# Attention stage of a hybrid decoder trunk: TensorE's products and turnings pinned to the program's order, new planner costs, k turned ahead of q

## The chip, the cores and the metric

The kernel runs on one core of a Trainium2 chip. The metric is the device time of one execution in microseconds (us), as the median of several runs. Lower is better.

## What is computed

Two layers on x of 512 positions by 1024. Each layer is a gated feed-forward block, a mixer and another gated feed-forward block; the mixer of layer 0 is a causal differential attention with 8 heads, that of layer 1 a chunked spatial gate. All is float32. Only the attention matters here:

```python
def _diff_attention(h, w_in, w_out, q_norm, k_norm, lq1, lk1, lq2, lk2, subln, lam_init):
    q, k, v = jnp.split(h @ w_in, ...)                 # 512 x 1024 each
    q = _rmsnorm(q.reshape(B, S, H, 2, d), q_norm) * (d ** -0.5)   # d = 64, two halves a head
    k = _rmsnorm(k.reshape(B, S, H, 2, d), k_norm)
    for i in range(S // Q_BLOCK):                      # 4 blocks of 128 queries
        L = (i + 1) * Q_BLOCK
        s = jnp.einsum('bqhcd,bkhcd->bhcqk', q_blk, k[:, :L])
        p = jax.nn.softmax(jnp.where(mask, s, -jnp.inf), axis=-1)
        a = p[:, :, 0] - lam * p[:, :, 1]
        outs.append(jnp.einsum('bhqk,bkhe->bqhe', a, v[:, :L]))
    o = _rmsnorm(o, subln) * (1.0 - lam_init)
    return o.reshape(B, S, DIFF_V_WIDTH) @ w_out
```

## The kernel before, in words

x lies transposed in SBUF, 8 tiles of 128 x 512. To keep float32 precision every operand is cut into a high and a low half, and each product is made of three matmuls (high x high, low x high, high x low): `mm3`, which calls `matmul` at L135. The stages follow one another: feed-forward f0, attention, f1, f2, spatial gate, f3.

The attention stage (`attention`, from L594) consists of tasks, each a Python generator that issues some instructions and then yields what it thinks they cost. For a pair of heads `hp` there is a projection of q and k (`qk_block`: 96 matmuls of 512 columns through `project`, which yields after every six), a norm (`qk_norm`), and for every head h:

- `qk_turn` (task t): q and k of the head are turned by TensorE, four 128 x 128 turnings into one bank of PSUM for q and one for k. ScalarE and VectorE copy them out as high and low halves, two copies on ScalarE for q and four for k.
- `scores` (s, once for each block i of 128 queries): for each of the two halves `cc` one bank, two matmuls of 128 to 512 columns and, after those of both halves, one that adds the mask; then a maximum (L740) and its scaling (L742) on VectorE, an exponential (L747) on ScalarE, and the combination of both halves (L752 to L754) on VectorE.
- `turn` (e): the combined block is turned, i + 1 turnings; ScalarE copies it out.
- `values` (p): products with v.
- `head_norm` (n) and `head_turn` (o): the head's norm and the turning of its output.

Two blocks of v (`v_block`) and the out-projection (`out_part`, task w, one for a pair of heads, 48 matmuls of 512 columns) use the same banks `pp` as the projections. PSUM has 8 banks: 4 `pp`, 3 `ps` in a ring (for turnings and scores), 1 `po` (for the values).

The order in which the program issues all this comes from a planner, `interleave`. It goes through the list of tasks and takes the first whose conditions hold and whose time has come by its own clock; the list has all tasks of the heads first, in the order p, e, s for each block, and the projections last. A condition "<s0.1" means that the task was issued; one without "<" that its whole chain of work is done by the planner's clock. HOP is what it adds between engines. The costs stand in the yields. If nothing is ready, the clock jumps on. For a score step the condition reads

```python
tasks.append((f"s{h}.{i}", [f"t{h}"] + [f"<e{t}" for t in at(2 * NT)]
              + [f"<s{t}" for t in at(1)], scores(h, i)))
```

The program's order is not the order that runs. A scheduler of the compiler sorts each engine's instructions by what it takes to be ready first. Only an instruction on which `tc.keep_in_program_order` is called stays behind the instruction that precedes it on its engine in the program. `matmul` calls it while the list `fixed` is not empty. That is so in the feed-forward stages (`ffn` appends to it), and not in the attention stage; there `scores` pins the mask products and all but the first of its four products by hand. `Weights.use` splits weights into halves up to three half blocks ahead and issues their loads on SP's queue.

Of the kernel before, what the change touches and what calls it, by code (L numbers as in the profile page):

```python
# [17 lines left out]
P = 128  # L18
S = 512
NT = S // P  # L20
D = 1024
# [29 lines left out]
RSTD_AT = (3, 5, 3, 3)  # L51
STEPS = ("A0 t0 h0 B0", "A1 t1 h1 B1", "P1 A2 t2 A3 Q5", "P6 B2 B3 r3 h2 h3")
FIRST_STEPS = ("", "A0 t0 h0 B0", "A1 t1 h1 B1", "A2 B2", "P1 A3 B3 r2 r3 Q5", "P6 r4 r5 h2 h3 h4 h5")
HOP = 0.2
END = "end"


# [1 line left out]
def kernel(  # L59
# [23 lines left out]
    nc = tc.nc  # L83
# [9 lines left out]
    def bank(name, tag="ps"):  # L93
# [4 lines left out]
    ident = const.tile([P, P], F32, name="ident")  # L98
    make_identity(nc, ident)
    ident_b = const.tile([P, P], BF16, name="ident_b")  # L100
    make_identity(nc, ident_b)
    mask_b = const.tile([P, P], BF16, name="mask_b")
    nc.gpsimd.memset(mask_b, 0.0)
    nc.gpsimd.affine_select(
        out=mask_b, in_=mask_b, compare_op=ALU.is_ge, fill=MASK, base=0,
# [24 lines left out]

    fixed = []

    def matmul(ps, stationary, moving, start, stop, more=False):

        mm = nc.tensor.matmul(ps, stationary, moving, start=start, stop=stop, skip_group_check=more)  # L135
        if fixed:
            tc.keep_in_program_order(mm)

    def mm3(ps, sh, sl, mh, ml, start, stop, more=False):
        matmul(ps, sh, mh, start, False, more)  # L140
# [425 lines left out]
            else:  # L566
                state[name] = t + HOP if wait is True else max(now, wait or 0.0)

    def project(weights, p, nm, norm, rr, taken):


        ps = [bank(f"{nm}p{n}", "pp") for n in range(NT)]

        def products(k, n):
            wh, wl = weights.parts[p + k // 2]
            c0, t0 = slice(k % 2 * 512, (k % 2 + 1) * 512), slice(n * P, (n + 1) * P)
            mm3(ps[n], norm.xh[k][:, t0], norm.xl[k][:, t0], wh[:, c0], wl[:, c0], k == 0, k == KT - 1)

        for k in range(KT - 2):
            if k % 2 == 0:  # L580
                yield from weights.use(p + k // 2)
            for n in range(NT):
                products(k, n)
                if n % 2 == 1:
                    yield 1.3, [], False
        if not rr:
            rr["r"] = norm.rstd()
        yield from weights.use(p + 3)
        for n in range(NT):
            products(KT - 2, n)  # L590
            products(KT - 1, n)
            yield 1.3, taken(n, ps[n]), False

    def attention(norm, nxt):  # L594
        with ExitStack() as c:
# [21 lines left out]
            srcs, where = [], {}  # L617
# [6 lines left out]
            weights = Weights(srcs)  # L624
# [3 lines left out]
            def qk_block(hp):  # L628

                nm = f"qk{hp}"  # L630
                ssqs[hp] = stat.tile([P, NT, 8], F32, tag="ssq", name=nm + "ssq")

                def taken(n, ps):
                    sq = stat.tile([P, S], F32, tag="sq", name=f"{nm}sq{n}")
                    nc.scalar.activation(sq, ps, AF.Square)
                    qks[hp, n] = a2.tile([P, 512], F32, tag="qk", name=f"{nm}n{n}", bufs=QK_BUFS)
                    nc.scalar.activation(qks[hp, n], ps, AF.Copy)
                    nc.vector.reduce_sum(ssqs[hp][:, n, :], sq.rearrange("p (g d) -> p g d", d=HD), axis=AX.X)
                    return [("A", 1.0), ("D", 0.6)]

                yield from project(weights, where["qk", hp], nm, norm, rr, taken)

            def v_block(b):

                vts[b] = a2.tile([P, NT, 512], F32, tag="vt", name=f"vt{b}", bufs=2)

                def taken(n, ps):
                    nc.scalar.activation(vts[b][:, n, :], ps, AF.Copy, scale=rr["r"][:, n:n + 1])
                    return [("A", 0.6)]

                yield from project(weights, where["v", b], f"v{b}", norm, rr, taken)

            def qk_norm(hp):
                nm = f"qk{hp}"
# [38 lines left out]
            def qk_turn(h):  # L693
                nm, hp, hh = f"qk{h}", h // 2, h % 2
                qs, khs, kls = stacks[h % 2]
                for j in (hh, 2 + hh):
                    pt = bank(f"{nm}t{j}")
                    for n in range(NT):
                        nc.tensor.transpose(pt[:, n * P:(n + 1) * P], qks[hp, n][:, j * P:(j + 1) * P], ident)
                    for c, own in enumerate(rows):  # L700
                        other = rows[1 - c]
                        if j < 2:
                            nc.scalar.activation(qs[c][own], pt[own], AF.Copy)
                            nc.vector.tensor_tensor(qs[c][other], pt[own], f32(qs[c][own]), op=ALU.subtract)
                        else:
                            nc.scalar.activation(khs[c][own], pt[own], AF.Copy, scale=kg[own])
                            nc.scalar.activation(khs[c][other], pt[own], AF.Copy, scale=kg[own])
                            nc.vector.scalar_tensor_tensor(
                                kls[c][own], pt[own], kg[own], f32(khs[c][own]), op0=ALU.mult, op1=ALU.subtract
                            )  # L710
                    if j < 2:
                        yield 0.44, [("A", 1.1), ("D", 1.4)], False
                    else:
                        yield 0.44, [("A", 2.2), ("D", 1.4)], END

            def scores(h, i):

# [7 lines left out]
                pss = [bank(f"{nm}s{i}{cc}") for cc in range(2)]  # L725
                for cc in range(2):
                    for ks in (khs, kls):
                        mm = nc.tensor.matmul(
                            pss[cc][:, :L], qs[cc][:, i * P:L], ks[cc][:, :L], start=ks is khs, stop=False
                        )  # L730
                        if cc > 0 or ks is kls:
                            tc.keep_in_program_order(mm)
                for cc in range(2):
                    tc.keep_in_program_order(
                        nc.tensor.matmul(pss[cc][:, i * P:L], ident_b, mask_b, start=False, stop=True)
                    )
                for cc in range(2):
                    ps = pss[cc]
                    mx = stat.tile([P, 2], F32, tag="mx", name=f"{nm}m{i}{cc}", bufs=8)
# [15 lines left out]
                es[h, i] = ee[0]  # L755
                yield (
                    (0.5, 0.54, 0.76, 0.97)[i],
                    [("D", 0.7 + 0.27 * i), ("A", 0.86 + 0.22 * i), ("D", 0.4), ("D", 0.25 + 0.13 * i)], END,
                )

            def turn(h, i):
                nm, L = f"a{h}", (i + 1) * P
                e = es.pop((h, i))
                pt = bank(f"{nm}at{i}")
                for j in range(i + 1):
                    nc.tensor.transpose(pt[:, j * P:(j + 1) * P], e[:, j * P:(j + 1) * P], ident)
                at = a2.tile([P, L], F32, tag=f"at{i}", name=f"{nm}atT{i}", bufs=1)
                nc.scalar.activation(at, pt[:, :L], AF.Copy)
                ats[h, i] = at
                yield 0.11 * (i + 1), [("A", 0.25 + 0.09 * i)], END  # L770

            def values(h, i):
                at = ats.pop((h, i))
                if i == 0:
                    ocs[h] = bank(f"a{h}o", "po")
                for j in range(i + 1):
                    nc.tensor.matmul(
                        ocs[h][:, i * P:(i + 1) * P], at[:, j * P:(j + 1) * P],
                        vts[h // 4][:, j, h % 4 * P:(h % 4 + 1) * P],
                        start=(j == 0), stop=(j == i),  # L780
                    )
                yield 0.22 * (i + 1), [], END

# [22 lines left out]
            def head_turn(h):  # L806
                nm, on = f"a{h}", ons.pop(h)
                pt = bank(nm + "ot")
                for n in range(NT):
                    nc.tensor.transpose(pt[:, n * P:(n + 1) * P], on[:, n, :], ident)  # L810
                oh = a2.tile([P, S], F32R, tag="oh", name=nm + "oh", bufs=O_BUFS)
                ol = a2.tile([P, S], F32R, tag="ol", name=nm + "ol", bufs=O_BUFS)
                nc.scalar.activation(oh, pt, AF.Copy, scale=sg)
                nc.vector.scalar_tensor_tensor(ol, pt, sg, f32(oh), op0=ALU.mult, op1=ALU.subtract)
                outs[h] = (oh, ol)
                yield 0.44, [("A", 0.57), ("D", 0.66)], END

            def out_part(hp):
                last = order[-1] == ("w", hp)
                for m in range(KT):  # L820
# [9 lines left out]
                    nc.vector.tensor_tensor(x[m], pt, x[m], op=ALU.add)  # L830
                    if last:
                        nxt.add(m)
                        yield 1.3, [("D", 0.6), ("A", 1.1), ("D", 1.3)], False
                    else:
                        yield 1.3, [("D", 0.6)], False

            tasks = []
            for hp in range(4):
# [17 lines left out]
            for w, i in order:  # L856
                if w == "w":
                    tasks.append((f"w{i}", [f"o{2 * i}", f"o{2 * i + 1}"] + prev, out_part(i)))
                else:
                    tasks.append((f"{w}{i}", prev, qk_block(i) if w == "qk" else v_block(i)))  # L860
                prev = [f"{w}{i}"]
            interleave(tasks)

    def gmlp(norm, nxt):
        with ExitStack() as c:
# [230 lines left out]
```

## Time and profile before

| | us |
|---|---|
| median of 3 runs | 1932.28 (1931.55 to 1933.58) |
| the profiled execution, whole time | 1931.58 |
| its span in the trace | 1929.9 |
| TensorE busy in the span | 1913.3 |
| VectorE busy | 1329.0 |
| ScalarE busy | 902.2 |
| attention stage, first to last product | 251.9 |

Engines: PE is TensorE's matmuls, PEld its weight loads, DVE VectorE, ACT ScalarE. A product's busy time is longer than its distance to the next one, since products are pipelined; the distance between two starts tells the pace. Numbers ahead of a row of the timeline are its start and its duration in us, counted from the span's start. Names are those of the program: a2s are the scores of head 2, qk2t the turned q or k of head 2, k1l the low half of the k of an odd head, qk2p the projection of the third pair (heads 4 and 5).

### The profile page before, as it was taken

What the parts mean: (1) busy time and instruction counts of PE and PEld (TensorE: products, weight loads), DVE (VectorE), ACT (ScalarE), POOL (GpSimd) and SP (SyncE); (2) the same over time, 40 slices, a digit from 0 to 9 for tenths busy, and PEclk for the clock granted to TensorE, in tenths of its full rate; (3) what the DMA queues carried; (4) which work ended last, traced back from release to release, by engine and by line L of the source; (5) the groups of instructions that cost most, each with busy time, mean ns of one, the idle gap of its engine ahead of it and who ended that gap; (6) DMA issues with size and microseconds to landing.
All of it is one profiled execution on the core that took longest, in us unless ns stands there. A gap on an engine that the chain in (4) does not pass through costs nothing.

```text
span 1929.9 us, 29295 instructions
## 1 busy us (share of the span) xinstructions
PE 1913.3 (99%) x11490; PEld 1701.5 (88%) x11490; DVE 1329.0 (69%) x2151; ACT 902.2 (47%) x1394; POOL 63.2 (3%) x81
## 2 busy tenths in 40 slices
PE   8999999999999999999999999999999999999999
PEld 7889898877778889899889999988888888999997
DVE  7857574778888957566696666755595569665763
ACT  6535353566764635354454444543332245343541
POOL 0000000000000000000000000000000000000000
PEclk9999999999999999999999999999999999999999
DMA  6354562422122455554435545543333234454542
GB/s 211 97 143 134 131 149 80 133 66 66 55 66 88 104 137 129 137 145 125 120 99 140 142 133 142 133 135 110 107 109 95 88 109 105 136 137 137 133 125 82
DMA packets 88985, 227.51 MB, mean 118 GB/s; under 512 B 10000, under 2 KB 43152, under 8 KB 88848
## 3 DMA queue, kind: packets, MB, share of 16 engines
q1 hardware_dynamic: 78768, 188.95, 31.0%
q0 software_dynamic: 10080, 36.70, 11.5%
q8 instruction: 90, 1.47, 0.3%
q14 instruction: 47, 0.39, 0.1%
HBM read 223.52 MB, written 2.10 MB: 117 GB/s over the span
## 4 chain that ended last, share of the span: by engine, by line
PE 95%; DVE 2%; ACT 2%; issue 0%; DMA 0%; SPq 0%; ACTq 0%
PE f3dp L135 6%; PE f0dp L135 6%; PE f2dp L135 6%; PE f1dp L135 6%; PE gup L135 5%; PE gop L135 5%; PE f0p L135 3%; PE aop L135 2%; PE f3p L135 2%; PE f2p L135 2%; PE gv0p L135 1%; PE qk0p L135 1%; PE qk1p L135 1%; PE gv1p L135 1%; PE gv2p L135 1%; PE gv3p L135 1%
## 5 line engine op out<-in xcount | busy, mean ns | idle before, releaser
L490 DVE SCALAR_TENSOR_TENSOR x<-f3dp,x 128x512 f32<-128x512 f32 x32 | 22.1, 691 | 60.5 <-PE f3dp L135 60.5
L490 DVE SCALAR_TENSOR_TENSOR x<-f1dp,x 128x512 f32<-128x512 f32 x32 | 22.1, 690 | 49.2 <-PE f1dp L135 49.2
L490 DVE SCALAR_TENSOR_TENSOR x<-f2dp,x 128x512 f32<-128x512 f32 x32 | 22.1, 689 | 49.2 <-PE f2dp L135 49.2
L490 DVE SCALAR_TENSOR_TENSOR x<-f0dp,x 128x512 f32<-128x512 f32 x32 | 22.1, 690 | 48.8 <-PE f0dp L135 48.8
L987 DVE TENSOR_TENSOR x<-gop,x 128x512 f32<-128x512 f32 x24 | 16.5, 689 | 20.0 <-PE gop L135 20.0
L967 ACT ACTIVATE gh<-gut 128x512 fp32r<-128x512 f32 x16 | 10.1, 633 | 42.9 <-DVE gut L966 42.9
L830 DVE TENSOR_TENSOR x<-aop,x 128x512 f32<-128x512 f32 x32 | 21.3, 683 | 2.0 <-PE aop L135 1.9
L962 DVE TENSOR_TENSOR gst<-gs,bs 128x512 f32<-128x512 f32 x16 | 11.0, 686 | 8.8 <-PE gs L957 8.8
L957 PEld LDWEIGHTS gs<-wT,gv 128*128 128x128 f32 x128 | 16.1, 191 | 0.9
L957 PE MATMUL gs<-wT,gv 128*128 128x128 f32 x128 | 16.2, 274 | 0.0
L907 ACT ACTIVATE gv<-gv 128x512 f32<-128x512 f32 x16 | 10.1, 629 | 12.4 <-DVE gv L906 12.3
L926 DVE TENSOR_TENSOR gut<-gup,n4rbs 128x512 f32<-128x512 f32 x16 | 11.0, 685 | 6.6 <-PE gup L135 6.6
L927 ACT ACTIVATE gut<-gut,sm 128x512 f32<-128x512 f32 x16 | 11.5, 719 | 6.7 <-DVE gut L926 6.6
L968 DVE TENSOR_TENSOR gl<-gut,gh 128x512 fp32r<-128x512 f32 x16 | 11.0, 687 | 4.2 <-ACT gh L967 4.2
L266 POOL DMA_DIRECT2D f1w2b<-in_gate_up_dram x1 | 0.9, 865 | 358.7 <-DVE f1w2t L262 358.7
L942 DVE SCALAR_TENSOR_TENSOR gv<-gv,lnmv,lng 128x512 f32<-128x512 f32 x16 | 11.5, 742 | 1.5 <-DMA lng<-in_ln_g_dram 1.5
L943 DVE SCALAR_TENSOR_TENSOR gv<-gv,lny,lnb 128x512 f32<-128x512 f32 x16 | 11.6, 746 | 1.3 <-DMA lnb<-in_ln_b_dram 1.3
L266 POOL DMA_DIRECT2D f3w2b<-in_gate_up_dram x1 | 0.9, 877 | 354.2 <-DVE f3y L356 354.2
L467 ACT ACTIVATE f1g<-f1g 128x512 f32<-128x512 f32 x9 | 5.7, 633 | 14.3 <-DVE f1g L465 14.3
L467 ACT ACTIVATE f3g<-f3g 128x512 f32<-128x512 f32 x9 | 5.7, 633 | 14.3 <-DVE f3g L465 14.3
L467 ACT ACTIVATE f2g<-f2g 128x512 f32<-128x512 f32 x9 | 5.7, 633 | 14.3 <-DVE f2g L465 14.3
L966 DVE TENSOR_TENSOR gut<-gut,gst 128x512 f32<-128x512 f32 x16 | 11.0, 689 | 0.7
(20715 smaller groups left out, 8029.5 us busy)
## 6 DMA issues: line engine op xcount, KB each, us to landing
f0d<-in_down_dram SPq DMA_DIRECT2D x48, 192.0 KB, 2.5
f1d<-in_down_dram SPq DMA_DIRECT2D x48, 192.0 KB, 2.5
f2d<-in_down_dram SPq DMA_DIRECT2D x48, 192.0 KB, 2.5
f3d<-in_down_dram SPq DMA_DIRECT2D x48, 192.0 KB, 2.7
f0gu<-in_gate_up_dram SPq DMA_DIRECT2D x10, 512.0 KB, 4.9
f1gu<-in_gate_up_dram SPq DMA_DIRECT2D x8, 512.0 KB, 3.5
f2gu<-in_gate_up_dram SPq DMA_DIRECT2D x8, 512.0 KB, 3.6
f3gu<-in_gate_up_dram SPq DMA_DIRECT2D x8, 512.0 KB, 3.6
```

The source lines that it names most:

```text
L135: mm = nc.tensor.matmul(ps, stationary, moving, start=start, stop=stop, skip_group_check=more)
L467: nc.scalar.activation(g[:, 2:, :], g[:, 2:, :], AF.Silu)
L490: nc.vector.scalar_tensor_tensor(x[m], pt, 0.5, x[m], op0=ALU.mult, op1=ALU.add)
L830: nc.vector.tensor_tensor(x[m], pt, x[m], op=ALU.add)
L926: nc.vector.tensor_tensor(ut, ps, rr["rb"], op=ALU.mult)
L927: nc.scalar.activation(ut, ut, AF.Gelu, bias=sm[:, C_BU + c:C_BU + c + 1])
L942: nc.vector.scalar_tensor_tensor(vv, vv, mv[:, n, 0:1], gr, op0=ALU.subtract, op1=ALU.mult)
L943: nc.vector.scalar_tensor_tensor(vv, vv, rr["y"][:, n:n + 1], lr, op0=ALU.mult, op1=ALU.add)
L957: nc.tensor.matmul(ps[:, n * P:(n + 1) * P], v32[n][:, c * P:(c + 1) * P], wT[:, g, :], start=True, stop=True)
L962: nc.vector.tensor_tensor(t.rearrange("p (n t) -> p n t", t=P), ps.rearrange("p (n t) -> p n t", t=P), bs[:, g, :].unsqueeze(1).broadcast_ ...
L966: nc.vector.tensor_tensor(ut, ut, t, op=ALU.mult)
L987: nc.vector.tensor_tensor(x[m], pt, x[m], op=ALU.add)
```

## The change

It pins every matmul and every turning of the attention stage to the program's order: `fixed` is filled around `interleave(tasks)`, products and turnings all go through `pin`. The planner's HOP and the costs in the yields of the attention stage grow, the six matmuls of a projection to STEP = 1.37. `qk_turn` turns k first and then q. No instruction is added or taken away.

```diff
-HOP = 0.2
+HOP = 0.3
+STEP = 1.37
@@
-    def matmul(ps, stationary, moving, start, stop, more=False):
-
-        mm = nc.tensor.matmul(ps, stationary, moving, start=start, stop=stop, skip_group_check=more)
+    def pin(mm):
+
         if fixed:
             tc.keep_in_program_order(mm)
+
+    def matmul(ps, stationary, moving, start, stop, more=False):
+
+        pin(nc.tensor.matmul(ps, stationary, moving, start=start, stop=stop, skip_group_check=more))
+
+    def turned(out, src):
+        pin(nc.tensor.transpose(out, src, ident))
@@ qk_block
-                    return [("A", 1.0), ("D", 0.6)]
+                    return [("A", 1.25), ("D", 0.7)]
@@ qk_turn
-                for j in (hh, 2 + hh):
+                for j in (2 + hh, hh):
                     pt = bank(f"{nm}t{j}")
                     for n in range(NT):
-                        nc.tensor.transpose(pt[:, n * P:(n + 1) * P], qks[hp, n][:, j * P:(j + 1) * P], ident)
+                        turned(pt[:, n * P:(n + 1) * P], qks[hp, n][:, j * P:(j + 1) * P])
@@
-                        yield 0.44, [("A", 1.1), ("D", 1.4)], False
+                        yield 0.44, [("A", 1.3), ("D", 1.4)], END
                     else:
-                        yield 0.44, [("A", 2.2), ("D", 1.4)], END
+                        yield 0.44, [("A", 2.5), ("D", 1.5)], False
@@ scores
-                        mm = nc.tensor.matmul(
-                            pss[cc][:, :L], qs[cc][:, i * P:L], ks[cc][:, :L], start=ks is khs, stop=False
-                        )
-                        if cc > 0 or ks is kls:
-                            tc.keep_in_program_order(mm)
+                        matmul(pss[cc][:, :L], qs[cc][:, i * P:L], ks[cc][:, :L], ks is khs, False)
@@
-                    [("D", 0.7 + 0.27 * i), ("A", 0.86 + 0.22 * i), ("D", 0.4), ("D", 0.25 + 0.13 * i)], END,
+                    [("D", 0.9 + 0.27 * i), ("A", 1.28 + 0.22 * i), ("D", 0.5), ("D", 0.28 + 0.15 * i)], END,
@@ out_part
-                        yield 1.3, [("D", 0.6), ("A", 1.1), ("D", 1.3)], False
+                        yield STEP, [("D", 0.7), ("A", 1.25), ("D", 1.45)], False
                     else:
-                        yield 1.3, [("D", 0.6)], False
+                        yield STEP, [("D", 0.7)], False
@@ end of attention
+            fixed.append(1)
             interleave(tasks)
+            fixed.pop()
```

The turnings and products of `turn`, `values` and `head_turn` are changed in the same way as those of `qk_turn` and `scores`, and `qk_block` and `v_block` hand STEP to `project`.

## Rows read from the trace of the kernel before

**Rows 1.** The page: busy time of the engines, and the chain's shares by engine.

```profile
PE 1913.3 (99%) x11490; PEld 1701.5 (88%) x11490; DVE 1329.0 (69%) x2151; ACT 902.2 (47%) x1394; POOL 63.2 (3%) x81
PE 95%; DVE 2%; ACT 2%; issue 0%; DMA 0%; SPq 0%; ACTq 0%
```

**Rows 2.** Busy time in the attention stage; columns as in the first line.

```profile
core 0: us, PE busy (x) PEld busy (x) DVE busy (x) ACT busy (x) POOL busy (x), PEclk, DMA share, GB/s
356.20:608.10 251.90, 246.35 (x1306) 199.63 (x1306) 202.30 (x571) 160.44 (x318) 0.00 (x0) 1.00 0.22 68
```

**Rows 3.** The chain in order of time: start, us, unbroken run of one group.

```profile
420.25 0.77 PE a0at L766 x7
...
432.91 6.85 PE qk1p L135 x30
...
441.59 8.16 PE qk2p L135 x36
```

**Rows 4.** Products of projections (L135) in the four score groups: busy (count).

```profile
394.90:417.86 22.96, 16.83 (x64) 11.38 (x64) 1.00 0.22 70
457.18:479.55 22.37, 16.45 (x62) 10.85 (x61) 1.00 0.23 69
503.37:526.00 22.63, 17.57 (x66) 11.53 (x65) 1.00 0.24 71
538.78:565.32 26.54, 15.67 (x55) 9.55 (x54) 1.00 0.20 60
```

**Rows 5.** Timeline of TensorE in the second group: score products (L728) and masks.

```profile
460.19 0.36 PE L728 MATMUL a2s<-k0h,q0h 128*128 128x256 f32 x1 [1.33 <-DVE k1l L708]
...
461.45 0.38 PE L728 MATMUL a2s<-k0h,q0l 128*128 128x256 f32 x1
...
461.79 0.28 PE L735 MATMUL a2s<-mask_b,ident_b 128*128 128x128 bf16 x2
...
463.73 0.34 PE L728 MATMUL a2s<-k0h,q0l 128*128 128x384 f32 x1
...
466.75 0.50 PE L728 MATMUL a2s<-k0h,q0l 128*128 128x512 f32 x1
```

**Rows 6.** Timeline of VectorE and ScalarE in the same stretch.

```profile
462.05 0.42 DVE L740 TENSOR_REDUCE a2m<-a2s 128x1 f32<-128x256 f32 x1
...
462.58 0.20 DVE L742 TENSOR_SCALAR a2m<-a2m,qk1rq 128x1 f32<-128x1 f32 x1
...
466.79 1.22 DVE L128 TENSOR_TENSOR aqk31s0l<-aqk31r,aqk31s0h 128x1024 fp32r<-128x1024 f32 x1
...
462.88 0.57 ACT L747 ACTIVATE a2e<-a2s,a2m,qk1rq 128x256 f32<-128x256 f32 x1 [1.04 <-DVE a2m L742]
```

**Rows 7.** Busy time of all engines in the second group, columns as in rows 2.

```profile
457.18:479.55 22.37, 21.04 (x110) 16.08 (x108) 19.47 (x61) 16.33 (x40) 0.00 (x0) 1.00 0.23 69
```

**Rows 8.** Timeline of the turnings of heads 2 and 3 and their copies.

```profile
449.60 1.03 PE L699 MATMUL qk2t<-ident,qk1n 128*128 128x128 f32 x8
450.23 0.59 ACT L703 ACTIVATE q0h<-qk2t 64x512 fp32r<-64x512 f32 x1 [2.10 <-PE qk2t L699]
...
451.41 0.69 ACT L707 ACTIVATE k0h<-qk2t,kg 64x512 fp32r<-64x512 f32 x1
...
453.74 0.63 PE L699 MATMUL qk3t<-ident,qk1n 128*128 128x128 f32 x4
```

**Rows 9.** Timeline at the stage's end: the last turning and its two copies.

```profile
596.93 0.63 PE L810 MATMUL a7ot<-ident,a7on 128*128 128x128 f32 x4
597.60 0.69 ACT L813 ACTIVATE a7oh<-a7ot,sg 128x512 fp32r<-128x512 f32 x1 [0.30 <-PE a7ot L810]
...
598.48 0.74 DVE L814 SCALAR_TENSOR_TENSOR a7ol<-a7ot,sg,a7oh 128x512 fp32r<-128x512 f32 x1
```

**Rows 10.** Timeline of TensorE at the start of the kernel.

```profile
5.67 0.63 PE L135 MATMUL f0p<-n0x0l,w00wh 128*128 128x512 f32 x1
6.10 0.63 PE L135 MATMUL f0p<-n0x0h,w00wl 128*128 128x512 f32 x1
...
9.49 0.40 PE L135 MATMUL f0p<-n0x1l,w00wh 128*128 128x512 f32 x1
```

## What the change was predicted to do

> **What bounds the kernel now.** The page comes first: TensorE is busy 99% of the span and carries 95% of the chain that ended last [rows 1]. The second view is the busy time of the attention stage, whose products run from 356.2 to 608.1 us: 251.9 us, TensorE busy 246.35 of them [rows 2]. That looks as if no more than 5.5 us were to be had. So the third thing to read is the pace of unbroken runs: 36 products of 512 columns in 8.16 us, 0.227 each, and seven turnings in 0.77, 0.11 each [rows 3]. The stage has 768 products of 512 columns (174.1 us), 176 turnings and 160 value products at 0.11 (37), and 32 score steps for which the planner's own figures give 2.77 per head (22.2). That is 234 us, so 18 of the 252 are waits and joints, and 18 is the most that any order of TensorE's work could give back.
>
> The Trainium skill says the same of such a row: in "Trainium Kernel Development and Optimization", section "Performance Expectations", it calls matmul busy time a bad metric because matmuls are pipelined. By the busy row the most to be gained would be 5.5 us; by the pace it is 18, and the trace agrees with the page.
>
> The fourth view is what TensorE does while the scores run, in four groups (heads 0 and 1, 2 and 3, 4 and 5, 6 and 7). Each of the first three takes 22.4 to 23.0 us, and between the score steps lie 64, 62 and 66 products of the projections (55 of the out-projection in the last, 26.5 us) [rows 4]. So a group holds only 5.5 us of score work; the rest is filler.
>
> **The order that the change fixes.** The program's order has to be read out of the planner. At each step it takes the first task in its list that is ready, and the projections stand last in the list. A score step of a head needs its turned halves, and of the score step before it only that it was *issued* (the "<" in its conditions). So as soon as a pair's halves count as ready, s0 to s3 of one head are issued behind one another, and soon those of the other head. Banks of PSUM don't occur in the planner. Worked through with the new costs, the first pair reads: 48 products of v0, turnings k, q, k, q, 24 products, four score steps, 6 products, four score steps, 12 products, then the turnings of e0, e1 and so on among 6 to 24 products each. The other pairs are alike (with the last: four score steps, p4 and e5, four score steps, then 48 products). The old costs give nearly the same (36 products before the first turning, no filler at all between the two heads). The trace bears the reading out at places where nothing waits: 36 products before the turnings of head 2, and exactly 30 between those of a0 and a1's outputs [rows 3]. But in the score groups the trace holds 62 to 66 products where the program's order has none. In the kernel before only the later products of a score step are pinned; projections float into its waits. The change forbids that.
>
> **Score groups.** A score step takes two banks of a ring of three. Its second half therefore waits until the exponential of the step before has freed its first bank. The round can be seen in the trace: second half at 461.45, the masks at 461.79, maximum at 462.05, its scaling at 462.58, exponential at 462.88 for 0.57, and the second half of the next step at 463.73: 2.28 us [rows 5, 6]. The next round is 3.02 us [rows 5], but foreign work stands in it and behind it: squares on ScalarE, weight splits of 1.22 on VectorE [rows 6]. Without these I take 1.75, 2.28, 2.5 and 2.6 us for the four rounds of a head (an estimate: the round that is seen, its maximum and exponential shortened or lengthened by the width). For eight steps from first product to last mask that is 1.85 + 2.28 + 2.5 + 2.6 + 1.75 + 2.28 + 2.5 + 0.7 = 16.5 us; VectorE is busy 19.5 of 22.4 us in such a group [rows 7]; without the three splits in it 15 to 16 stay. That will stretch the rounds here and there, and I take 17.5. The bounds are 15 (VectorE's share alone) and 22.4 (as now, with the foreign work in it).
>
> Of the 22.96, 22.37 and 22.63 us of the first three groups, all filler but 6 products is pushed behind the group: 58 x 0.227 = 13.2, 12.7 and 13.6 us. What is left of them is 9.8, 9.7 and 9.0. In their place stands 17.5: 52.5 - 28.5 = **+24.0** (bounds +16.5 and +38.7). In the last group 26.54 - 55 x 0.227 = 14.1 is left; in its place come two runs of four steps (1.85 + 2.28 + 2.5 + 0.7 = 7.3 each), 30 value products and turnings (3.3) and 0.5 for their banks: 18.5, **+4.4** (bounds +4 and +12.6). Behind the waiting score product all of TensorE is queued; nobody else waits for the filler, which is why nothing gives the time back.
>
> **Turnings, k ahead of q.** No instruction is added. There are four turned blocks and three banks, so the last block (q of the second head) waits for the first bank, which is now that of k: four copies on ScalarE at 0.69 (the first copy begins 0.63 after the turning does in the trace [rows 8]), about 3.45 us after the start, and 1.3 us of other turnings lie in between. So 2.15 us are bare. In the trace the fourth block starts 4.14 us after the first [rows 8], and 11 floated products cover it; with that wait 2.85 would be bare. I take 2.4, of which 0.4 are there now: **+8** for four pairs (bounds +6.8 and +10). That k comes first helps no one: a score step needs both.
>
> **The end.** After the last turning (596.93) the halves of head 7 are done at 599.2 [rows 9]: 2.3 us. Turning (0.44) and the three products of head 6 that may run (0.68) leave **+1.2**; now floated products cover it.
>
> **The rest.** The costs and STEP change landmarks only; products stand there that wait for nothing. The loads on SP and the weight splits move with the projections by a few steps. Three halves are split ahead, and 24 products of one half are 5.4 us of cover. Fewer joints and small waits elsewhere: from -8 (nearly half of the 18 us) to +2; I take -1.
>
> **Sum.** 24.0 + 4.4 + 8 + 1.2 - 1 = +36.6 us on the profiled execution's own 1931.58: **1968**. (Its span is 1929.9; the median of the runs shown, 1932.28, lies 0.7 above it.) Bounds: +20 and +63, 1951 to 1995.
>
> **Rivals.**
> *The clock falls too: 1987, chance 0.10.* In the first microseconds of the kernel products of 512 columns stand 0.43 us apart instead of 0.227 [rows 10], which is the lower of the two levels (1.2 against 2.4 GHz), until about 9.5 us: ten products at 0.2 too much, 2 us lost. If four groups with bare waits brought this level back, each would lose between those 2 us and its own work once more (6.9): +8 to +28, I take +18. Against it: the granted clock is 1.00 throughout the stage although waits of 1.3 us occur in it [rows 2, 5]. The Trainium skill, "TensorE: Matmul & The Clock Gate", section "A second HAM failure mode: psum-queue depth-cycling", describes just this: short idling between groups while PSUM banks are cycled lets the clock go back and forth. No run here shows it.
>
> *The order saves waits: 1922, chance 0.12.* Of the 18 us of waits and joints, over half could go if the planner's order put the products where the waits are. It decides in the score groups: filler between score steps must be 1.3 us or more in each round. For it: the costs of the softmax steps grow, which makes the planner hold back what depends on them, and a wait like that of 1.33 us for a bank [rows 5], which 24 products ahead of it don't cover now, could be met by an order that knows the longer copies. Against it: a successor score step depends on the issue alone, so longer costs put no filler between them.
>
> *Nothing that can be measured: 1932, chance 0.08.* If the pins bound little, because the order was nearly the program's already, or if bare waits (2.4 a pair) were paid back by joints. Against it stand the 62 to 66 floated products.
>
> **How the numbers follow.** A measurement of this kernel can tell about 0.2% (3.9 us) from no change. Forecast 0.70 and the clock 0.10 are slower: 0.80. Faster 0.12, same 0.08. The two slower cases hold 8 in 10, so the range is 1951 to 1995.
>
> **What would show it.** Right: the attention stage is about 37 us longer and the rest of the kernel unchanged; eight score steps in 16 to 20 us with 6 products of a projection between them, rounds of 1.7 to 2.8 us; TensorE's busy share in these groups falls well under 90%, with waits of scores on the exponential; the fourth turning waits 2 us or more. Wrong: projections still between the score steps, or rounds near 1 us (then the ring of banks is not what sets them), or a granted clock under 1.00.

## The result, and the profile after

The changed kernel takes **2018.31 us** (median of five, 2017.17 to 2019.78) beside 1931.78 for the kernel before: a ratio of 1.0448 (95% interval 1.0436 to 1.046). The forecast was 1968 with a range of 1951 to 1995. It is slower, as forecast, but by 86.5 us instead of 36.6.

The page of the changed kernel, engine row and chain, and the busy time of its attention stage from its first product to the first of the next stage (columns as in [rows 2]; matmuls now have line 141, turnings 144):

```profile
PE 1950.4 (97%) x11490; PEld 1727.1 (86%) x11490; DVE 1333.7 (66%) x2151; ACT 902.7 (45%) x1394; POOL 63.2 (3%) x81
PE 93%; DVE 4%; ACT 2%; issue 1%; DMA 0%; SPq 0%; ACTq 0%; DVEq 0%
...
356.71:695.48 338.77, 283.96 (x1305) 225.36 (x1304) 207.56 (x572) 162.70 (x319) 0.00 (x0) 0.85 0.17 50
```

The stage grew from 251.75 us (356.26 to 608.01, the same two instructions) to 338.77: **+87.0, the whole difference**. It holds the same work as in [rows 2], but TensorE's busy time in it rose by 37.6 us and the mean granted clock fell from 1.00 to 0.85.

What TensorE waited for in the stage, in the changed kernel and then in the kernel before (total, times, longest; the first rows of each list):

```profile
PE a4s L141 <- ACT a4e L748: 5.3, 3, 2.9
PE a2s L141 <- ACT a2e L748: 4.8, 3, 2.0
PE qk7t L144 <- DVE k0l L715: 4.6, 1, 4.6
PE qk1t L144 <- DVE k0l L715: 4.6, 1, 4.6
PE a0s L141 <- ACT a0e L748: 4.6, 3, 2.2
PE qk5t L144 <- DVE k0l L715: 4.1, 1, 4.1
PE qk3t L144 <- DVE k0l L715: 4.1, 1, 4.1
```

```profile
PE a0s L728 <- DVE k1l L708: 1.3, 1, 1.3
PE a2s L728 <- DVE k1l L708: 1.3, 1, 1.3
PE a6s L728 <- ACT a6e L747: 1.1, 1, 1.1
```

Added up over the stage the waits are 54.8 us after and 5.2 before. So of the 87 us some 50 are new waits, scores on the exponential and the fourth turning on VectorE, and some 37 are the same work done more slowly.

The four score groups, and (last row) the window of the second pair from its first turning to its first score product:

```profile
404.05:428.45 24.40, 15.50 (x55) 9.67 (x54) 12.92 (x48) 11.99 (x31) 0.00 (x0) 0.64 0.08 23
488.94:513.47 24.53, 15.55 (x56) 10.03 (x54) 14.12 (x50) 11.13 (x32) 0.00 (x0) 0.58 0.07 22
554.34:579.72 25.38, 15.26 (x56) 9.76 (x54) 17.81 (x67) 12.20 (x34) 0.00 (x0) 0.63 0.14 42
612.33:637.34 25.01, 16.83 (x79) 12.21 (x78) 16.60 (x65) 12.95 (x36) 0.00 (x0) 0.71 0.07 22
475.85:488.94 13.09, 9.03 (x41) 7.36 (x40) 6.98 (x10) 8.78 (x13) 0.00 (x0) 0.87 0.14 41
```

A group is longer than in [rows 4] although its 62 to 66 products of projections are gone: between the heads stand six, and none before the second head's end. The clock, 1.00 in [rows 4], is 0.58 to 0.71 here. Six products of a projection between two heads show the level, with starts 0.42 to 0.43 us apart, as at the start of the kernel [rows 10]. The two rows behind them are the changed kernel's stretch around these products, with a granted clock of 0.50, and the kernel before in its first products:

```profile
499.76 0.63 PE L141 MATMUL qk2p<-aqk21s1l,n1x6h 128*128 128x512 f32 x1
500.18 0.63 PE L141 MATMUL qk2p<-aqk21s1h,n1x6l 128*128 128x512 f32 x1
500.61 0.63 PE L141 MATMUL qk2p<-aqk21s1h,n1x7h 128*128 128x512 f32 x1
...
492.90:516.80 23.90, 16.96 (x49) 11.22 (x49) 13.63 (x51) 9.44 (x27) 0.00 (x0) 0.50 0.01 4
...
5.00:9.40 4.40, 4.33 (x10) 3.28 (x11) 2.87 (x6) 3.40 (x8) 0.00 (x0) 1.00 0.90 321
```

So [rows 10] show the lower level by their pace alone: the profile gives a granted clock of 1.00 there. In the attention stage both agree, 0.50 with products 0.43 us apart.

Against the terms of the prediction, in us:

| | forecast | measured |
|---|---|---|
| score groups, filler pushed out (99.3 in all, where 42.6 was left) | +28.4 | +56.7 |
| turnings to first score (13.59, 13.10, 14.58, 13.59; before 7.6, 7.6, 8.65, 7.75) | +8 | +23.2 |
| products right behind the groups, the first four to seven 0.43 apart instead of 0.227 | none | +5.0 |
| the end | +1.2 | +2 |
| rest | -1 | 0 |

### The profile page after: what moved, and what is told of

Same layout as the page of the kernel before. It is cut to its first block, busy times and chain, and to the rows that moved or that the text cites. A ratio compares the mean times of both kernels' runs of the same rounds, so it can differ in the third digit from the quotient of the medians.

```text
span 2016.6 us, 29292 instructions
## 1 busy us (share of the span) xinstructions
PE 1950.4 (97%) x11490; PEld 1727.1 (86%) x11490; DVE 1333.7 (66%) x2151; ACT 902.7 (45%) x1394; POOL 63.2 (3%) x81
## 4 chain that ended last, share of the span: by engine, by line
PE 93%; DVE 4%; ACT 2%; issue 1%; DMA 0%; SPq 0%; ACTq 0%; DVEq 0%
PE f3dp L141 6%; PE f1dp L141 6%; PE f2dp L141 6%; PE f0dp L141 6%; PE gup L141 4%; PE gop L141 4%; PE f0p L141 3%; PE aop L141 2%; PE f3p L141 2%; PE f2p L141 2%; PE v0p L141 1%; PE qk2p L141 1%; PE v1p L141 1%; PE qk3p L141 1%; PE gv0p L141 1%; PE qk0p L141 1%
## 5 line engine op out<-in xcount | busy, mean ns | idle before, releaser
L969 ACT ACTIVATE gh<-gut 128x512 fp32r<-128x512 f32 x16 | 10.1, 629 | 30.5 <-DVE gut L968 30.5
```

## The experiments

The kernel before was timed beside every experiment and stays at 1931.7 to 1931.9 us, so the times of the experiments are set against the changed kernel's 2018.31 too. A time that has neither an interval nor a ratio beside it is one execution; five executions of the changed kernel lie 2.6 us apart. Two theories of the 50 us that were missed stood at the start: the rounds and turnings are longer than I took them even at full clock, or TensorE's clock falls in the bare waits and stretches everything.

**The pins alone.** The planner's old costs and the old order of turning, with the pins:

```diff
-HOP = 0.3
-STEP = 1.37
+HOP = 0.2
+STEP = 1.3
@@ qk_turn
-                for j in (2 + hh, hh):
+                for j in (hh, 2 + hh):
```

The costs in the yields are those of the kernel before, too.

> The pins alone, on the planner's old costs and with q turned ahead of k. Theory (bare waits in the fixed order, costs and k-first beside the point): 2008 to 2028 us, granted clock in the four score groups well under 0.8, eight score steps in 22 us or more, no projections between them. Rival (the new costs, or k ahead of q, carry the loss): under 1975 us.

2010.61 us, with a stage of 330.75. The pins carry 79 of the 87 us; new costs and k ahead of q add 7.7 more. No product of a projection lies in the first three groups; they take 23.3, 21.5 and 23.6 us at a granted clock of 0.56 to 0.64, so the second is a little under the 22 us that were expected. The fourth turning's gap (from the start of the last turning ahead of it to its own) is 2.8 to 2.9 us with q first, against 4.3 to 4.8 with k first; the rows of waits above give about 0.2 less for the same gaps, 4.1 to 4.6.

**No pins.** New costs and k first, the pins out, the score products pinned by hand as before:

```diff
-            fixed.append(1)
             interleave(tasks)
-            fixed.pop()
@@ scores
-                        matmul(pss[cc][:, :L], qs[cc][:, i * P:L], ks[cc][:, :L], ks is khs, False)
+                        mm = nc.tensor.matmul(
+                            pss[cc][:, :L], qs[cc][:, i * P:L], ks[cc][:, :L], start=ks is khs, stop=False
+                        )
+                        if cc > 0 or ks is kls:
+                            tc.keep_in_program_order(mm)
```

> The new costs and k ahead of q without the pins (the products of a score step pinned by hand as in the kernel before). Theory: 1925 to 1942 us, granted clock 1.00 through the attention stage, 50 or more projection products in each score group. Rival (costs or k-first carry part of the loss): 1950 us or more.

1933.12 us, ratio 1.0008 (0.9998 to 1.0018). Costs and turning order cost nothing that can be measured as long as products may float into the waits: the four groups hold 65, 65, 66 and 58 products of projections.

**Only the filler free.** All pins stay, except on the products of the projections (`project`, in the same way) and of the out-projection:

```diff
+    def loose(ps, sh, sl, mh, ml, start, stop):
+        nc.tensor.matmul(ps, sh, mh, start=start, stop=False)
+        nc.tensor.matmul(ps, sh, ml, start=False, stop=False)
+        nc.tensor.matmul(ps, sl, mh, start=False, stop=stop)
@@ out_part
-                        mm3(pt, wh[:, c0], wl[:, c0], oh, ol, k == 0, k == 1)
+                        loose(pt, wh[:, c0], wl[:, c0], oh, ol, k == 0, k == 1)
```

> The changed kernel with the products of the projections and of the out-projection not pinned (768 of 512 columns), everything else pinned: scores, turnings, values. Theory (what the pins cost is the filler that can no longer float into the waits): 1928 to 1945 us, granted clock 1.00, 50 or more projection products in each score group. Rival (the order of the turnings and values among the scores carries part of the loss): over 1955 us.

1933.33 us, ratio 1.0009 (0.9999 to 1.0018), clock 1.00. So it isn't the order of turnings, scores and value products that costs; it is that the filler is held out of their waits. That is the mechanism of the forecast, shown. The groups hold 65, 65, 66 and 61 products again and take 23.0, 22.6, 22.6 and 27.8 us. The fourth turning comes as late as in the changed kernel (6.06 and 5.55 us after the first one in the first two pairs, against 6.04 and 5.52), but TensorE waits for it 0.4 to 0.5 us only: filler covers the rest.

**Products into the waits.** Products with zero weights, added to an open bank of a projection: 17 ahead of the fourth turning, five ahead of a second half of the scores. A bank is open for all four turnings, and for the scores of the first two pairs and of the first head of the third (17 of the 28 waits there). They change no value and add 34.7 us of TensorE work (153 more products at 0.227), laid where it would wait:

```diff
+                    if hh == 1 and j < 2:
+                        idle_work(17, zero, norm.xh[0])
@@ scores
                 for cc in range(2):
+                    if cc == 1 and (i or hh):
+                        idle_work(5, zero, norm.xh[0])
```

> The changed kernel with products of zero weights put into the waits: 17 ahead of the fourth turning of a pair, 5 ahead of the second half of a score step (from the second step on), accumulated into the bank of the projection that is open, so its sums don't change. They reach the turnings of all pairs and the score groups of pairs 1 and 2 (and the first head of pair 3). Theory that the clock carries much of what the prediction missed: granted clock 1.00 in these stretches, score groups of pairs 1 and 2 from 24.4 to 18 to 20 us, turning windows from 13.6 to about 11.9 us, 1988 to 2000 us in all. Rival (the rounds are set by VectorE and ScalarE whatever the clock): groups stay at 23 us or more, 2004 to 2014 us.

1998.76 us: more work, 19.5 us less time. The groups of the first two pairs in this kernel:

```profile
480.36:501.15 20.79, 17.99 (x91) 12.65 (x89) 14.04 (x50) 11.02 (x32) 0.00 (x0) 1.00 0.08 26
402.00:422.90 20.90, 17.83 (x90) 12.55 (x89) 12.93 (x48) 11.88 (x31) 0.00 (x0) 1.00 0.08 26
```

The clock is 1.00 there and the group 3.5 to 3.7 us shorter. In the stage the mean clock rises from 0.85 to 0.96 and the stage falls by 19.1 us; carried on to 1.00 in proportion, the clock is worth some 26 us (an estimate: 19.1 x 0.15 / 0.11). But 20.8 is not 17.5: at full clock, with the added products in them, the rounds are still longer than forecast. Both theories hold a part.

**VectorE's order in a round.** One round of the changed kernel, from the second half of one score step to that of the next (TensorE, VectorE and ScalarE):

```profile
491.96 0.38 PE L141 MATMUL a2s<-k0h,q0l 128*128 128x256 f32 x1 [2.04 <-ACT a2e L748]
...
492.57 0.42 DVE L741 TENSOR_REDUCE a2m<-a2s 128x1 f32<-128x256 f32 x1 [1.12 <-PE a2s L141]
...
492.91 0.15 DVE L753 RECIPROCAL a2cf<-a2sums 128x1 f32<-128x1 f32 x1
492.98 0.41 DVE L741 TENSOR_REDUCE a2m<-a2s 128x1 f32<-128x256 f32 x1
493.31 0.27 DVE L754 TENSOR_SCALAR a2cf<-a2cf,a2sums,nlam 128x1 f32<-128x1 f32 x1
493.49 0.20 DVE L743 TENSOR_SCALAR a2m<-a2m,qk1rq 128x1 f32<-128x1 f32 x1
...
493.79 0.56 ACT L748 ACTIVATE a2e<-a2s,a2m,qk1rq 128x256 f32<-128x256 f32 x1 [1.44 <-DVE a2m L743]
...
494.49 0.69 PE L141 MATMUL a2s<-k0h,q0l 128*128 128x384 f32 x1 [1.46 <-ACT a2e L748]
```

Between the first half's maximum (492.57) and its scaling (493.49), for which the exponential waits, VectorE does three other things. In [rows 6] scaling follows maximum after 0.53; here it is 0.92. The experiment pins the scaling ahead of the second half's maximum:

```diff
-                    nc.vector.reduce_max(mx[:, 0:1], ps[:, :L], axis=AX.X)
+                    top = nc.vector.reduce_max(mx[:, 0:1], ps[:, :L], axis=AX.X)
+                    if cc == 1:
+                        tc.keep_in_program_order(top)
@@
-                    nc.vector.tensor_scalar(mx[:, 1:2], mx[:, 0:1], sc, -1.0, op0=ALU.mult, op1=ALU.mult)
+                    tc.keep_in_program_order(
+                        nc.vector.tensor_scalar(mx[:, 1:2], mx[:, 0:1], sc, -1.0, op0=ALU.mult, op1=ALU.mult)
+                    )
```

> The changed kernel with VectorE's order in a score step held to the program's: the scaling of the first half's maximum before the maximum of the second half. Theory (between maximum and scaling VectorE does the other half's maximum and parts of the step before, 0.4 to 0.7 us in each of 28 rounds, while the next score products wait): 1998 to 2006 us, score groups of the first three pairs 20 to 22 us instead of 24.4 to 25.4. Rival (the rounds are set by the low clock and the exponentials): 2012 to 2020 us, groups over 23.5 us.

2007.33 us, 11 less, between the two expectations. The first two groups take 20.5 and 21.3 us, the clock still 0.73 and 0.59 (the third and fourth 22.7 and 22.4):

```profile
404.03:424.50 20.47, 14.02 (x54) 8.88 (x53) 13.54 (x48) 12.32 (x31) 0.00 (x0) 0.73 0.10 27
484.87:506.20 21.33, 15.18 (x55) 9.90 (x54) 14.67 (x50) 11.41 (x32) 0.00 (x0) 0.59 0.09 26
```

The same edit on the kernel before:

> The kernel before with the scaling of a maximum ahead of the other half's maximum on VectorE, as in the run on the changed kernel. Theory (in the kernel before the filler covers these rounds, so a shorter round is worth little): 1929 to 1933 us. Rival (score rounds end last there too, 0.4 us in 28 rounds): 1918 to 1926 us.

1931.83 us, ratio 1.0 (0.999 to 1.001): there the rounds are covered by filler, and their length is free.

**Both at once.** The two edits above together:

> Edit: the changed kernel with both single remedies at once: products with zero weights in the waits (alone 1998.76 us, groups of 21.0 us) and the scaling ahead of the second half's maximum on VectorE (alone 2007.33 us, groups of about 20.4 and 21.4). Theory: the two excesses over the 17.5 us that were predicted for a group are separate, one the clock and one VectorE's order; then a group of the first pairs falls to 17 to 18.5 us and the time to 1982 to 1989. Rival: both act on the same wait, so that TensorE's own work in a round (score products, mask and five zero products, about 2.2 us) is late next: groups of 20 us or more, 1993 to 2000.

1991.34 us. The groups of the first two pairs:

```profile
402.48:421.96 19.48, 17.36 (x90) 12.80 (x89) 13.41 (x48) 12.00 (x30) 0.00 (x0) 1.00 0.09 28
479.41:498.71 19.30, 17.21 (x90) 12.87 (x89) 14.69 (x50) 11.41 (x32) 0.00 (x0) 1.00 0.08 28
```

That lies between the theories: 19.5 + 11.0 would be 30.5, together they give 27.0. So of a group's excess of 7 us over 17.5, about 3.5 is the clock, 1.5 VectorE's order at full clock, and 2 stays. The zero products themselves may be part of these 2 us: TensorE waits only 1.9 and 2.1 us in these two groups, so its own work, the added products with it, sets most of the rounds.

The last pair of this run shows a round without them, since no bank is open there. Its first head, from the first score product to the products with v, runs at full clock; the second row is the same head in the changed kernel, and the rows behind it are the second halves:

```profile
589.61:597.35 7.74, 4.26 (x26) 2.62 (x24) 5.68 (x19) 4.97 (x13) 0.00 (x0) 1.00 0.23 69
...
612.33:621.64 9.31, 5.50 (x25) 3.37 (x24) 5.46 (x19) 5.24 (x14) 0.00 (x0) 0.68 0.18 59
...
591.93 0.38 PE L142 MATMUL a6s<-k0h,q0l 128*128 128x256 f32 x1 [1.35 <-ACT a6e L765]
...
594.20 0.44 PE L142 MATMUL a6s<-k0h,q0l 128*128 128x384 f32 x1
...
596.65 0.50 PE L142 MATMUL a6s<-k0h,q0l 128*128 128x512 f32 x1 [1.11 <-ACT a6e L765]
```

The forecast had 7.3 us for such a run of four steps, and rounds of 2.28 and 2.5; here they are 2.27 and 2.45. At full clock and with the scaling first, then, the forecast's rounds come out for this head; for the other heads no run shows them bare at full clock.

**The fourth turning: ScalarE's copies in order.** In the changed kernel ScalarE copies blocks of other banks between the four copies of k:

```profile
477.18 0.68 ACT L714 ACTIVATE k0h<-qk2t,kg 64x512 fp32r<-64x512 f32 x1
477.88 0.59 ACT L710 ACTIVATE q0h<-qk2t 64x512 fp32r<-64x512 f32 x1
478.38 0.67 ACT L713 ACTIVATE k1h<-qk3t,kg 64x512 fp32r<-64x512 f32 x1
479.06 0.68 ACT L713 ACTIVATE k0h<-qk2t,kg 64x512 fp32r<-64x512 f32 x1
```

Here all its copies of turned blocks are pinned to the program's order (`copied` calls `tc.keep_in_program_order`):

```diff
-                            nc.scalar.activation(khs[c][own], pt[own], AF.Copy, scale=kg[own])
+                            copied(nc.scalar.activation(khs[c][own], pt[own], AF.Copy, scale=kg[own]), h)
```

> The changed kernel with ScalarE's copies of the turned blocks pinned to the program's order too (four of k, two of q, for each head). Theory (ScalarE takes copies of other blocks between the four of the first bank, which doubles the wait of the fourth turning): that wait falls from 4.3 to 4.8 us to 2.1 to 2.6 us; with it the low clock behind the wait goes too, 2000 to 2005 us. If the clock falls all the same: 2006 to 2011 us. Rival (the wait hangs on VectorE's subtractions): the wait stays over 4 us and the time at 2015 to 2020.

2016.53 us, 1.8 less, which is within the 2.6 us by which executions of the changed kernel differ; the gaps are 3.9 to 4.5 us instead of 4.3 to 4.8. The theory fell, the rival holds, and this kernel's timeline shows why (turnings, copies, VectorE's low halves):

```profile
475.21 0.68 ACT L720 ACTIVATE k0h<-qk2t,kg 64x512 fp32r<-64x512 f32 x1 [0.74 <-PE qk2t L144]
...
475.90 0.68 ACT L721 ACTIVATE k0h<-qk2t,kg 64x512 fp32r<-64x512 f32 x1
476.62 0.74 DVE L722 SCALAR_TENSOR_TENSOR k0l<-qk2t,kg,k0h 64x512 fp32r<-64x512 f32 x1 [0.89 <-ACT k0h L721]
477.40 0.68 ACT L720 ACTIVATE k0h<-qk2t,kg 64x512 fp32r<-64x512 f32 x1 [0.81 <-DVE k0l L722]
478.09 0.68 ACT L721 ACTIVATE k0h<-qk2t,kg 64x512 fp32r<-64x512 f32 x1
...
478.81 0.76 DVE L722 SCALAR_TENSOR_TENSOR k0l<-qk2t,kg,k0h 64x512 fp32r<-64x512 f32 x1 [1.45 <-ACT k0h L721]
...
479.71 0.63 PE L144 MATMUL qk3t<-ident,qk1n 128*128 128x128 f32 x4 [3.67 <-DVE k0l L722]
```

ScalarE and VectorE take turns on the bank of k: two copies, VectorE's subtraction, two copies, the second subtraction, and only then the turning; 475.21 to 479.57 is 4.36 us. ScalarE, with nothing else in front of it, waits 0.81 us for a subtraction whose result it doesn't use. The Trainium skill, "PSUM — Partial Sum Buffer", section "PSUM bank collisions raise a hardware error", says that the compiler's scheduler makes instructions of different engines wait for each other where they touch the same bank in the same quarter of the partitions, reads of ScalarE and VectorE included. The rows agree on the turns, and go further: by the program the copy that waits 0.81 us reads the rows from 64 on, the subtraction the rows below 64. What put this wait there is not shown.

**A bank of its own for the fourth block.**

```diff
-                    pt = bank(f"{nm}t{j}")
+                    pt = bank(f"{nm}t{j}", "po" if hh and j < 2 else "ps")
```

> Edit: the changed kernel with the fourth turned block of a pair (q of the second head) in the bank of the values, which is free then, instead of the first of the ring of three. Theory: the fourth turning's wait of 4.3 to 4.8 us comes only from the bank of k, whose readers take turns; with a bank of its own the wait is gone, nothing else waits in its place, and the window from first turning to first score product falls from 13.1 to 14.6 us to 7.5 to 9: four times 5 to 6 less, 1994 to 2000. Rival: ScalarE's copies (twelve in a pair, 8 us) are what is late next, so that part of the wait moves behind the 24 products to the first score step or into the first group: 2003 to 2014.

2005.67 us, within the rival's range: 12.6 us less, where the theory gave 18 to 24. The first two pairs, each from first turning to first score and then the group:

```profile
390.91:398.11 7.20, 7.20 (x42) 6.26 (x40) 4.64 (x6) 6.72 (x10) 0.00 (x0) 1.00 0.25 77
398.11:425.20 27.09, 16.34 (x54) 10.45 (x53) 15.26 (x52) 13.94 (x34) 0.00 (x0) 0.57 0.07 21
473.06:480.27 7.21, 7.21 (x41) 6.25 (x40) 5.06 (x7) 6.44 (x10) 0.00 (x0) 1.00 0.24 73
480.27:507.20 26.93, 16.32 (x54) 10.41 (x53) 16.14 (x53) 13.37 (x36) 0.00 (x0) 0.56 0.07 20
```

The wait is gone from the turnings (13.1 to 13.6 us become 7.2), and the group behind is 2.4 to 2.7 us longer: ScalarE and VectorE are then still at work on the blocks of the second head, and the scores wait for them (1.9 us for the low half of its k, in each of these two groups). The clock falls all the same, with no wait of TensorE over 2.2 us in these two groups or ahead of them.

**Pins kept, waits planned for.** The planner holds each score step but the first of a pair back by 1 to 2 us and the fourth turning by 2, so that products of projections are issued there; q first, HOP 0.2, shorter softmax costs:

```diff
+                    if hh and j >= 2:
+                        t = yield 0, [], False
+                        yield 0, [], t + 2.0
@@ scores, ahead of a step
+                if i or hh:
+                    t = yield 0, [], False
+                    yield 0, [], t + (2.0, 1.0, 1.0, 2.0)[i]
```

> All pinned as in the changed kernel, but the planner is told of the waits: it holds a score step back by 1.0 or 2.0 us of its clock behind the step before, and the fourth turning by 2.0 (q first again, shorter softmax costs), so that 6 or 12 projection products stand in each wait in the program's order. Theory (not the pins cost, but the place of the filler): 1928 to 1950 us, granted clock 1.00 but for the last group, where filler runs out. Rival (a fixed order costs by itself, since real waits differ from the planner's): over 1970 us.

1951.77 us, ratio 1.0104 (1.0089 to 1.0119), a little over what I expected at most, but 66.5 of the 86.5 us are back without one pin taken off. Up to 7.7 of them can be q first and the costs, which is what the kernel with the pins alone gained on the changed one. What the stage still lacks is 20 us: its waits add up to 18.1 us instead of 5.2, and the rest is clock (0.97) and joints. The last group, where the filler has run out, holds 4.5 us of the waits, at a clock of 0.89:

```profile
569.80:602.00 32.20, 27.70 (x161) 21.28 (x160) 27.44 (x97) 17.96 (x47) 0.00 (x0) 0.89 0.18 49
```

With VectorE's order as well:

> Edit: the kernel with products of the projections planned into the waits (1951.77 us) and, on VectorE, the scaling of a first half's maximum pinned ahead of the second half's maximum, which alone took 11 us from the changed kernel (2018.31 to 2007.33). Theory: what is left of the loss, 20 us, lies largely in rounds that are still longer than the products put into them (waits of 0.9 to 1.5 us before second halves in all four groups, and the last group with hardly any filler left). Then shorter rounds give back about 0.5 us each where the wait is bare: 1942 to 1948. Rival: it lies in the joints, since the filler runs in pieces of six products of 1.47 us instead of 1.36, and in the turnings: then the order on VectorE gives nothing more, 1950 to 1953.

1949.91 us (1948.81 to 1951.0, two executions): the theory failed, and the time lies at the edge of the rival's 1950 to 1953. Where a round has its filler, a shorter round gives 1.9 us in all, which these few executions can't tell from nothing. That the rest lies in the joints, as the rival has it, is not shown. No version that was run beats the kernel before.

## Why the prediction was wrong in size and right in direction

**The bound and the order: right.** TensorE's order in the trace is the one worked out from the planner: 48 products of v0, turnings k, q, k, q, 24 products, four score steps, six products, four score steps. The rest of the kernel didn't change. The filler's pins are the cause, by the two kernels without them (1933.12 and 1933.33).

What failed is the price of the bare waits, in two terms, and the full clock that both terms took for granted.

**Score groups: the term that was mis-sized.** Its form held (filler out, bare rounds in); the 17.5 us for a group of the first three pairs measured 24.4 to 25.4, above even the upper bound of 22.4, and the 18.5 for the last 25.0. Two reasons, each with a run: the clock (about 3.5 us a group) and VectorE's order in a round (about 1.5). With both out of the way, and no zero products either, the one head that shows it takes what the forecast had (7.74 us for 7.3). I had taken the round from [rows 5, 6], where 0.53 us lie between maximum and scaling, and called the foreign work in the next round, 3.02 us, an exception. Bare, the rounds that I put at 2.28 and 2.5 us measure 2.53 and 3.47 (second halves at 491.96, 494.49 and 497.96, the last of them at the low level).

**Turnings: the step that failed.** "Four copies on ScalarE ..., about 3.45 us after the start ... So 2.15 us are bare." The block of k has two more readers, VectorE's subtractions, and on one bank they go in turns with the copies: the wait rows have 4.1 to 4.6 us bare, for a subtraction (k0l) that the forecast didn't count. The 2.85 that I worked out for q first, from a trace in which the fourth block's start could be seen [rows 8], measured 2.8 to 2.9. Counting the copies alone was the error: here the bank came free after its last reader, and [rows 8] shows ScalarE's rows only. The half us between 4.1 and 4.6 is a weight split of 1.06 us that stands on ScalarE ahead of the first copy in the first and the last pair:

```profile
390.66 1.06 ACT L128 ACTIVATE aqk10s1h<-aqk10r 128x1024 fp32r<-128x1024 f32 x1 [4.39 <-PE v0p L141]
```

After this wait, eight or so of the 24 following products also run at the lower level, about 1.7 us for a pair.

**The clock: a rival that should have been a part of the forecast.** I gave it 0.10 and 18 us on top (8 to 28), because the clock stayed at 1.00 in a stage that has waits of 1.3 us [rows 2, 5]; a clock under 1.00 stood among the signs of being wrong, and it came. But that row is one wait in a stretch full of products; the forecast itself emptied four stretches of 20 us and more of their filler. Forecast and rival weren't two cases: the bare waits of the first bring the second about, and where free filler or zero products stand in them the clock is 1.00 again. The page of the Trainium skill that I named there ("TensorE: Matmul & The Clock Gate", section "A second HAM failure mode: psum-queue depth-cycling") speaks of such short waits between groups as banks are cycled, and of a clock that goes back and forth. The trace agrees with it in the first, third and fourth groups, where the clock falls to 0.50, is back at 1.00 after the products between the heads, and falls again; in the second it stays at 0.50 from 492.90 to 516.80. Over the groups 0.58 to 0.71 is granted. The clock is worth some 26 us, in the groups, behind them and behind the turnings; that is less than the 37 us by which the work itself was slower, presumably because a part of it runs beside a round that lasts as long anyway.

**The sum.** Of the 50.4 us that were missed, 28.3 lie in the groups, 15.2 in the turnings, 5.0 behind the groups and the rest at the end. By causes, all of them estimates from the runs above: the clock 26, the longer bare wait of the fourth turning 9 (4 x 2.2), and the remaining 15 whatever is longer at any clock, of which VectorE's order explains 6 (4 x 1.5). What the other 9 are was not settled; the zero products, from which the clock's share is worked out, may have hidden a part of it, since they lengthen the rounds in which they outlast the wait.

**The end: nearly right** (+2 for +1.2), and the "-8 to +2" for joints elsewhere came to nothing.

## What to carry to other kernels

Before work is pinned, read from the trace what floats into each wait now, and price the wait that is left bare by all readers of the buffer it waits for, on every engine. If the pins empty TensorE in several waits in a row, take the lower clock into the forecast, as a result of the same step and not as an accident beside it. To keep an order by pins, the filler has to be planned into the waits: that, with q turned first again, brought back 66.5 of 86.5 us, and the kernel whose filler floats was still faster (1933.33).

## What was not expected of the hardware

The granted clock fell to 0.56 and 0.57 in groups in which TensorE never waited longer than 2.2 us at a time (the kernel with a fourth bank), with products 0.427 us apart instead of 0.227; adding 34.7 us of products with zero weights to the changed kernel took 19.5 us away. And in the rows of the turnings two engines that only read one bank of PSUM didn't do so side by side: ScalarE's copy of one half of the rows began only after VectorE's subtraction on the other half (0.81 us of waiting).
